# Low-part sums in columns of their own: matmuls of 348 columns in the full-width tiles of a hybrid decoder layer

## The chip, the cores and the metric

One core of a Trainium2 chip runs the program once. The metric is device microseconds of one execution, less is better. Of the engines, TensorE (PE) multiplies matrices into PSUM, VectorE (DVE) and ScalarE (ACT) do elementwise work, GpSimd (POOL) does little here, and SyncE (SP) starts transfers (DMA).

## The reference

One inference step of a decoder layer for a prompt of 512 tokens and 8 single-token samples, 520 tokens together, D = 1024, FFN width 2816, float32:

```python
mod = silu(c) @ w_ada + b_ada                    # shift, scale, gate, twice
h = _modulate(_rmsnorm(x, p["norm_pre_mix"]), sh_m, sc_m)
proj = h @ p["w_in"]                             # u | z | xBC | dt | gate_s5 | gate_ssd
ya = S5(u)           # complex diagonal state space: scan, GELU, half-GLU (w_glu)
yb = SSD(z, xBC, dt) # Mamba-2: conv, chunked scan, gated rmsnorm
merged = g_a * (ya @ p["w_branch_s5"]) + g_b * (yb @ p["w_branch_ssd"])
x = x + gt_m * _rmsnorm(merged @ p["w_out"], p["norm_post_mix"])
h = _modulate(_rmsnorm(x, p["norm_pre_ffn"]), sh_f, sc_f)
gu = h @ p["w_ffn_in"]
f = (jax.nn.silu(gu[..., :D_FF]) * gu[..., D_FF:]) @ p["w_ffn_out"]
x = x + gt_f * _rmsnorm(f, p["norm_post_ffn"])
```

The outputs are x for both groups and the new states of S5, SSD and the convolution.

## The kernel before

**The dense products.** Features lie on the 128 partitions, tokens along the free axis, in two halves of HT = 260. Weights and activations are float32, and each is split in a high part (`hi`, `whi`, of the type fp32r) and the rest (`lo`, `wlo`). A product is then three passes, hi x whi + lo x whi + hi x wlo. The helper `product` (L1148) makes them for one block of 128 input features (a k-step) of one tile of 128 output features: for a tile of full width six matmuls of 260 columns, three into each half's PSUM bank. The profile gives all of them one line, L722, that of the helper `mm` (L716), and shows fp32r as f32; `pm` is one of two pairs of main banks (2 x 512 words), `bank` one of four single banks for side work.

**The tiles.** The loop at L1068 goes through the tiles in a fixed list: u (8) and dt, the gates ga and gb (16), for each of four groups B, C, four xs and four z (40), glu (8), bs5 (8), bssd (8, with 16 k-steps), then w_out and the first FFN tiles for one half of the tokens at a time, 36 FFN tiles (fg, fu) in full width, six of the output product fo in full width with 22 k-steps, and the last two of them in halves. The pairs `pm` alternate. `evac` (L1376) reads a finished tile's sums, and is issued after the first k-step of the next tile: for gates, B, C and xs by a copy on ScalarE of all 520 columns (L696), for z and glu by an activation, for the others by VectorE.

**Weights.** A chunk of 1024 columns is fetched (`wload`), cast to `whi` on ScalarE, and its rest `wlo` made on VectorE (1.0 and 1.2 us in the profile), three chunks ahead at most.

**Side work.** S5, SSD, the modulation and the norms are generators that issue operations between k-steps (`tick`). They use VectorE, ScalarE, single banks and some matmuls.

**The order.** Every helper records its operation with an estimated cost. At the end `Plan.order` plays the recording through as a list schedule by longest way to the end, several times with perturbed priorities, and takes the best. Its result is the fixed order of instructions on each engine. The matmuls of a k-step stay together (`main`, L755).

**The end.** The last two fo tiles run in halves of 264 and 256 tokens (`cutp`), and `rstd_last` (L1645) spreads the last 256 reciprocal deviations over the partitions with two diagonal matrices of 128.

Of the kernel before, what the change touches and what calls it, by code (L numbers as in the profile page):

```python
# [16 lines left out]
NP, NS = 512, 8  # L17
T = NP + NS
HT = T // 2
KD = 8  # L20
# [29 lines left out]
class Root:  # L50
    """A tile: `get` gives the real one (it may be made late); `loc` names the memory it lies in."""
# [14 lines left out]
class Ap:  # L66
    """A view of a tile: its shape and addresses at once, the real view when the operation is issued."""
# [65 lines left out]
    def cells(self):  # L133
        """Partitions, and the set of words in one of them (bits of an integer)."""
# [20 lines left out]
def fold(dims):  # L155
    """The dimensions with neighbours joined where one stride serves both."""
# [21 lines left out]
# delay in us from the end of an operation to the start of one that waits for it  # L178
# [7 lines left out]
class Line:  # L186
    """The time of one engine: busy stretches, into whose gaps operations are put."""
# [24 lines left out]
class Plan:  # L212
    """Records operations with the memory they touch, and orders them for the engines."""
# [51 lines left out]
    def remake(self, loc, fn, words):  # L265
        """The memory `loc` gets a new tile: after everything that used the old one."""
# [8 lines left out]
    def order(self):  # L275
        """The best of some schedules: by the longest way to the end, then by latest starts."""
# [38 lines left out]
    def back(self):  # L315
        """Priorities from the schedule played backwards: the time from an operation's latest start to the end."""
# [35 lines left out]
    def play(self):  # L352
        """The course of the operations, each engine taking the most urgent of those that can start."""
# [69 lines left out]
    def shift(self, t, free, cand):  # L423
        """An operation of DVE that ACT may take at time t, where that is done sooner."""
# [32 lines left out]
class Arena:  # L457
    """One run of words in a tile of one type; blocks are cut out of it first fit."""
# [39 lines left out]
class Mem:  # L498
    """A fixed float32 arena, and slots whose type (float32 or float32r) is chosen when one is empty."""
# [10 lines left out]
    def find(self, n, dt, top):  # L510
        """The place for n words: an arena index (0 = the fixed one), or None."""
# [89 lines left out]
class Builder:  # L601
    def __init__(self, tc, I, O, sb, ps, dr):
# [10 lines left out]
        self.cutp = HT  # L613
# [6 lines left out]
        self.sg, self.ffh, self.ffl = {}, [], []  # L620
# [57 lines left out]
    def relu(self, o, a, s):  # L678
        """max(a + s, 0)"""
# [1824 lines left out]
```

## Time and profile before

| | |
|---|---|
| median of 3 runs | 1202.06 us (1200.11 to 1204.35) |
| span of the profiled execution (its own time isn't listed apart) | 1193.2 us |
| median less that span | 8.9 us |
| TensorE busy | 1168.8 us, 98%, 10182 matmuls |
| VectorE busy | 814.7 us, 68% |
| ScalarE busy | 576.3 us, 48% |
| mean granted TensorE clock | 0.998 |

Busy time of TensorE is the time in which a matmul is under way. Matmuls overlap at their ends, so what one costs in a stream is the distance from its start to the start of the next, and not its duration. A clock of 1.00 is 2.4 GHz, and half of it 1.2 GHz.

### The profile page before, as it was taken

To read this page: it belongs to the slowest core of one execution; us is meant where nothing else is said; L and a number is where in the kernel's file an instruction comes from. 1 tells how busy PE (TensorE), PEld (TensorE's weight loads), DVE (VectorE), ACT (ScalarE), POOL (GpSimd) and SP (SyncE) were. 2 spreads that over 40 slices of the span, in tenths; PEclk is the share of its full clock that TensorE was granted. 3 is DMA by queue.
4 is the path that set the end of the run, shared out by engine and by line. 5 is a ranking of instruction groups with operands and counts; after the bars stand their busy time and mean duration, and the time that the engine had idled before them with its cause. 6 is when DMAs were issued, how large, how long until landed. Compare 5 with 4: busy or idle time off the path is not lost.

```text
span 1193.2 us, 24814 instructions
## 1 busy us (share of the span) xinstructions
PE 1168.8 (98%) x10182; PEld 1124.5 (94%) x10182; DVE 814.7 (68%) x1651; ACT 576.3 (48%) x981; POOL 4.9 (0%) x32
## 2 busy tenths in 40 slices
PE   8999999999999999999999999999999899999998
PEld 6899898999999999999998989999999899999997
DVE  6898989997696877868885435499576673322236
ACT  6655444357487657847853323465223222222233
POOL 0000000000000000000000000000000000000000
PEclk9999999999999999999999999999999999999999
DMA  8838698667243343355545674344566663223244
GB/s 292 278 119 219 162 215 224 180 160 208 82 134 101 114 128 125 116 175 169 188 145 201 241 268 144 129 166 147 182 217 203 198 206 104 88 81 97 83 130 135
DMA packets 118066, 195.49 MB, mean 164 GB/s; under 512 B 45856, under 2 KB 68800, under 8 KB 115648
## 3 DMA queue, kind: packets, MB, share of 16 engines
q1 hardware_dynamic: 117952, 193.90, 52.9%
q8 instruction: 80, 1.31, 0.4%
q14 instruction: 34, 0.28, 0.1%
HBM read 165.81 MB, written 23.86 MB: 159 GB/s over the span
## 4 chain that ended last, share of the span: by engine, by line
PE 79%; DMA 9%; DVE 7%; issue 1%; SPq 1%; ACT 1%; DVEq 0%; ACTq 0%
PE pm L722 64%; PE bank L722 14%; DVE s L640 4%; DMA arena<-in_ssm 3%; DVE arena L640 2%; PE bank L734 2%; DMA s<-in_w_as 1%; DMA out_ssm_s<-arena 1%; SPq L712 1%; DVE wlo L640 1%; DMA s<-in_w_in 1%; DMA ud<-s 1%; DMA s<-s 1%; DVE s L663 1%; ACT s L696 0%
## 5 line engine op out<-in xcount | busy, mean ns | idle before, releaser
L722 PE MATMUL pm<-hi,whi 128*128 128x260 f32 (+1 forms) x1856 | 497.5, 289 | 5.9 <-DVE arena L640 3.7
L722 PE MATMUL pm<-lo,whi 128*128 128x260 f32 (+1 forms) x1856 | 483.4, 282 | 0.0
L722 PE MATMUL pm<-hi,wlo 128*128 128x260 f32 x1840 | 370.4, 283 | 0.0
L722 PEld LDWEIGHTS pm<-hi,whi 128*128 128x128 f32 (+1 forms) x1856 | 349.6, 188 | 17.4 <-issue 13.0
L722 PEld LDWEIGHTS pm<-lo,whi 128*128 128x128 f32 (+1 forms) x1856 | 349.1, 188 | 0.1
L640 DVE TENSOR_TENSOR wlo<-arena,whi 128x1024 fp32r<-128x1024 f32 (+1 forms) x157 | 188.8, 1203 | 146.7 <-ACT whi L696 144.9
L722 PEld LDWEIGHTS pm<-hi,wlo 128*128 128x128 f32 x1840 | 282.9, 188 | 0.0
L696 ACT CAST whi<-arena 128x1024 fp32r<-128x1024 f32 (+1 forms) x158 | 162.6, 1029 | 197.1 <-PE pm L722 180.2
L722 PE MATMUL pm<-s,whi 128*128 128x260 f32 (+2 forms) x1128 | 184.2, 283 | 0.0
L640 DVE TENSOR_TENSOR arena<-arena 128x512 f32<-128x512 f32 (+11 forms) x299 | 140.3, 494 | 49.8 <-DMA arena<-in_ssm 29.4
L722 PEld LDWEIGHTS pm<-s,whi 128*128 128x128 f32 x1128 | 156.2, 188 | 5.1 <-issue 4.2
L722 PE MATMUL pm<-s,wlo 128*128 128x260 f32 (+2 forms) x564 | 117.2, 283 | 0.0
L722 PEld LDWEIGHTS pm<-s,wlo 128*128 128x128 f32 x564 | 88.1, 188 | 0.0
L691 ACT ACT_TABLE_LOAD x63 | 80.8, 1283 | 10.3 <-DMA s<-acd 3.5
L722 PE MATMUL bank<-s,s 128*64 128x128 f32 (+5 forms) x672 | 75.8, 282 | 5.6 <-ACT s L696 4.4
L722 PEld LDWEIGHTS bank<-s,s 128*128 128x128 f32 (+2 forms) x672 | 61.3, 164 | 10.9 <-ACT s L696 5.3
L691 ACT ACTIVATE s<-s 128x520 f32<-128x520 f32 (+10 forms) x89 | 50.0, 570 | 38.3 <-DVE s L640 17.7
L691 ACT ACTIVATE arena<-pm 128x260 f32<-128x260 f32 (+3 forms) x44 | 21.2, 489 | 92.7 <-PE pm L722 85.7
L640 DVE TENSOR_TENSOR s<-arena,s 128x520 fp32r<-128x520 f32 (+5 forms) x60 | 56.5, 948 | 10.6 <-ACT s L696 10.4
L640 DVE TENSOR_TENSOR s<-s,arena 128x8 f32<-128x8 f32 (+6 forms) x138 | 48.6, 369 | 13.8 <-ACT s L691 12.7
L722 PE MATMUL bank<-hi,s 128*128 128x260 f32 x256 | 55.5, 285 | 0.0
L722 PE MATMUL pm<-hi,s 128*128 128x260 f32 x256 | 55.0, 285 | 0.0
(122 smaller groups left out, 1265.8 us busy)
## 6 DMA issues: line engine op xcount, KB each, us to landing
arena<-in_w_in SPq DMA_DIRECT2D x59, 512.0 KB, 3.7
arena<-in_w_fi SPq DMA_DIRECT2D x44, 512.0 KB, 4.4
arena<-in_w_ada SPq DMA_DIRECT2D x12, 1024.0 KB, 7.5
arena<-in_w_fo SPq DMA_DIRECT2D x20, 512.0 KB, 3.6
arena<-in_ssmT SPq DMA_DIRECT2D x16, 512.0 KB, 4.4
s<-acd SPq DMA_DIRECT2D x16, 512.0 KB, 4.3
arena<-in_w_bssd SPq DMA_DIRECT2D x16, 512.0 KB, 5.4
arena<-in_ssm SPq DMA_DIRECT2D x32, 256.0 KB, 3.8
```

The costliest lines, as they stand in the source:

```text
L640: self.op("V", .068 + self.fs(o) / 960, lambda: self.nc.vector.tensor_tensor(out=real(o), in0=real(a), in1=real(b), op=op), [o], [a, b, *a ...
L663: self.op("V", .068 + self.fs(o) / 960, lambda: self.nc.vector.tensor_tensor_scan(out=real(o), data0=real(a), data1=real(b), initial=0.0, ...
L691: self.op("A", c, lambda: self.nc.scalar.activation(real(o), real(a), f, bias=real(bias), scale=real(scale)), [o], [a, scale, bias], None ...
L696: self.op("A", c, lambda: self.nc.scalar.copy(real(o), real(a)), [o], [a])
L712: p = self.op("S", .475 if same else .65, lambda: self.nc.sync.dma_start(out=real(o), in_=real(a)), [o], [a], None, c)
L722: self.pe(c, lambda: self.nc.tensor.matmul(real(o), lhsT=real(l), rhs=real(r), start=start, stop=stop), [o], [l, r])
L734: self.pe(.108, lambda: self.nc.tensor.transpose(real(o), real(a), real(d)), [o], [a, d])
```

## The change

High and low parts of the activations are stored side by side, for each half 260 columns of high part and then 260 of low part (`xhl`). In a full-width tile of a kind in `WIDE` one matmul with `whi` takes all 260 high columns of a half and, in the same run, the first LA = 88 of its low columns: 348 columns. The sums of low columns don't add to those of the high ones; they stand in columns 260 to 347 of the same bank. The other 2 x 172 low columns of both halves are one matmul of 344 columns into a single bank, `lob`, taken from the four for side work. The matmuls with `wlo` stay at 260 columns. The 344s of a tile's first two k-steps are held back and come with the third's (in three tiles: the first's with the second's). `evac` of such a tile now copies the two low pieces out on ScalarE, adds the high sums to them on VectorE (520 columns), and goes on from that. For gates, B, C and xs this stands in place of the copy; for the rest it is added. u, dt, w_out and all tiles in halves keep their six matmuls (three in a half). The single bank is one for all tiles, and three are left for side work. Costs in the planner change, the last halves are 260 and 260, and the last deviations take three diagonal blocks. Many lines of the whole diff only drop comments; they are left out here.

```diff
+LA = 88
+WIDE = ("ga", "gb", "B", "C", "xs", "z", "glu", "bs5", "bssd", "fg", "fu", "fo")
...
-        self.cutp = HT
...
+        self.lob, self.late = None, []
...
     def mm(self, o, l, r, start=True, stop=True):
         n, m = self.fs(r), l.shape[-1]
         if l.dtype == F32R:
-            c = max(n / 2400, .111) if m > 32 else .048
+            c = max(n / 2400 + (.0114 if n < 300 else .0025), .112)
         else:
-            c = max(n * 4 / 2400, .216) * max(m, 32) / 128 + (.021 if m <= 64 else 0.0)
+            c = max(n * 4 / 2400 + .005, .224) * max(m, 32) / 128 + (.021 if m <= 64 else 0.0)
...
-        self.hi, self.lo = [rt(KD * T, n).rearrange("p (k t) -> p k t", k=KD) for n in ("hi", "lo")]
+
+        self.xhl = rt(KD * 2 * T, "xhl")
+        self.hl = self.xhl.rearrange("p (k a c t) -> p k a c t", k=KD, a=2, c=2)
...
-                    while len(self.banks) < 2:
+                    while not self.banks:
                         self.tick()
                         self.now += 0.3
-                    self.ring4 = [self.pm[0][:, 0], self.banks.pop(), self.pm[1][:, 0], self.banks.pop()]
+                    self.ring4 = [self.pm[0][:, 0], self.lob, self.pm[1][:, 0], self.banks.pop()]
                 if kind == "fo" and idx == 8 - NLAST and halves[0] == 0:
                     self.evac(*pend)
                     pend = None
-                    self.cutp = T - 256
...
+            wide = len(halves) == 2 and kind in WIDE
+            if wide and self.lob is None:
+                while not self.banks:
+                    self.tick()
+                    self.now += 0.3
+                self.lob = self.banks.pop()
...
-                    self.product(hi, lo, kk, pn, halves, k == 0, k == nk - 1, *rhs(k))
+                    self.product(hi, lo, kk, pn, halves, k == 0, k == nk - 1, rhs(k), wide,
+                                 k > (0 if (kind, idx) in (last, ("glu", 7), ("bssd", 7)) else 1))
                 if (kind, idx) == last:
                     if k == 0:
                         self.gelu()
-                    self.split(self.hi[:, k], self.lo[:, k], self.ub.v(KD, T)[:, k])
-                if (kind, idx) == ("glu", 7) and k < 7:
+                    for i in (k - 1,) * (k > 0) + (k,) * (k == 7):
+                        self.split(self.hl[:, i], self.ub.v(KD, T)[:, i])
+                if (kind, idx) == ("glu", 7):
                     if k == 0:
                         self.evac(*pend)
                         pend = None
-                    self.split(self.hi[:, k], self.lo[:, k], self.ub.v(KD, T)[:, k])
+                    else:
+                        self.split(self.hl[:, k - 1], self.ub.v(KD, T)[:, k - 1])
...
-    def product(self, hi, lo, k, p, halves, start, stop, xh, xl):
...
+    def product(self, hi, lo, k, p, halves, start, stop, x, wide=False, flush=True):
...
         wh, wl = [a[:, 128 * k:128 * k + 128] for a in (hi, lo)]
         self.group = []
-        for n in halves:
-            s = self.span(n)
-            self.mm(p[n][:, :s.stop - s.start], wh, xh[:, s], start=start, stop=False)
-            self.mm(p[n][:, :s.stop - s.start], wh, xl[:, s], start=False, stop=False)
-        for n in halves:
-            s = self.span(n)
-            self.mm(p[n][:, :s.stop - s.start], wl, xh[:, s], start=False, stop=stop)
+        if wide:
+            w = HT + LA
+            for n in halves:
+                self.mm(p[n][:, :w], wh, x[:, n].rearrange("p c t -> p (c t)")[:, :w], start=start, stop=False)
+            for n in halves:
+                self.mm(p[n][:, :HT], wl, x[:, n, 0], start=False, stop=stop)
+            self.late.append((self.lob[:, :2 * (HT - LA)].rearrange("p (a t) -> p a t", a=2), wh, x[:, :, 1, LA:], start, stop))
+            if flush:
+                for o, w, r, f, l in self.late:
+                    self.mm(o, w, r, start=f, stop=l)
+                self.late = []
+        else:
+            for n in halves:
+                for c in range(2):
+                    self.mm(p[n][:, :HT], wh, x[:, n, c], start=start and c == 0, stop=False)
+            for n in halves:
+                self.mm(p[n][:, :HT], wl, x[:, n, 0], start=False, stop=stop)
         self.main()
...
     def evac(self, kind, i, p, halves):
         pv = p[:, :, :HT] if len(halves) == 2 else None
         sp = lambda ap: ap.rearrange("p (a b) -> p a b", a=2)
+        lb = None
+        if len(halves) == 2 and kind in WIDE:
+            lb = self.mblk(T)
+            l2 = sp(lb.v(T))
+            self.acp(l2[:, :, LA:], sp(self.lob[:, :2 * (HT - LA)]))
+            self.acp(l2[:, :, :LA], p[:, :, HT:HT + LA])
+            self.vtt(l2, l2, pv, ADD)
+            pv = l2
+            p = l2
...
-            raw = self.mblk(T)
+            raw, lb = lb, None
             rv = raw.v(T)
-            self.acp(sp(rv), pv)
...
         elif kind in ("ga", "gb"):
-            b = self.mblk(T)
-            self.acp(sp(b.v(T)), pv)
+            b, lb = lb, None
...
     def rstd_last(self):
...
+        at = [(c0, 128), (c0 + 128, 128), (T - 128, HT - 256)]
...
+        self.vts(d[:, 2], self.ident, t[:, 2, 2:3], MULT)
...
```

On TensorE in the input projection (`pm_69`, `pm_70` are the two main pairs, `whi_71` to `wlo_75` weight buffers), two k-steps before:

```order
L722 MATMUL pm_69<-hi,whi_71 128x260
L722 MATMUL pm_69<-lo,whi_71 128x260
L722 MATMUL pm_69<-hi,whi_71 128x260
L722 MATMUL pm_69<-lo,whi_71 128x260
L722 MATMUL pm_69<-hi,wlo_74 128x260 x2
L722 MATMUL pm_70<-hi,whi_72 128x260
L722 MATMUL pm_70<-lo,whi_72 128x260
L722 MATMUL pm_70<-hi,whi_72 128x260
L722 MATMUL pm_70<-lo,whi_72 128x260
L722 MATMUL pm_70<-hi,wlo_75 128x260 x2
```

And in the change, around the third k-step of a gate tile, where the held matmuls of 344 columns come (`bank_66` is the bank `lob`):

```order
L724 MATMUL pm_70<-xhl,whi_72 128x348 x2
L724 MATMUL pm_70<-xhl,wlo_75 128x260 [waits DVE_49]
L724 MATMUL pm_70<-xhl,wlo_75 128x260
L724 MATMUL pm_70<-xhl,whi_72 128x348 x2
L724 MATMUL pm_70<-xhl,wlo_75 128x260 x2
L724 MATMUL pm_69<-xhl,whi_71 128x348 x2
L724 MATMUL pm_69<-xhl,wlo_74 128x260 x2
L724 MATMUL bank_66<-xhl,whi_71 128x344 [waits Activation_49]
L724 MATMUL bank_66<-xhl,whi_71 128x344 x2
L724 MATMUL pm_69<-xhl,whi_71 128x348 x2
L724 MATMUL pm_69<-xhl,wlo_74 128x260 x2
```

A k-step has five matmuls in place of six; three of 344 columns come together behind the third k-step's others, and the first of them waits for ScalarE.

On ScalarE at gate tiles, before (`s_16`, `s_18` are blocks of tokens, `arena` holds the fetched weights):

```order
L696 COPY s_16_997<-pm_69 128x520 [waits PE_49]
L696 CAST whi_71<-arena 128x1024 [waits DMAHW2_49]
L696 COPY s_13_579<-bank_65 128x256 [waits PE_49]
L696 COPY s_16_997<-arena 128x8x63 [waits DMAHW2_49,Activation_49]
L691 ACTIVATE s_13_579<-s_13_579 128x8x2 [waits DVE_49]
L696 COPY s_18_1108<-pm_70 128x520 [waits PE_49]
L691 ACTIVATE s_14_682<-s_14_682 128x130 [waits DMAHW3_49,DVE_49]
L696 CAST whi_72<-arena 128x1024 [waits DMAHW1_49]
```

In the change:

```order
L698 COPY s_16_776<-bank_66 128x2x172 [waits PE_49]
L698 COPY s_16_776<-pm_69 128x2x88
L698 CAST whi_71<-arena 128x1024 [waits DMAHW5_49]
L693 ACT_TABLE_LOAD [waits DMAHW4_49]
L693 ACTIVATE s_13_578<-s_13_578 128x130 [waits DVE_49]
L693 ACTIVATE s_13_578<-s_13_578 128x8x5 [waits DVE_49,Activation_49]
L693 ACTIVATE s_13_578<-s_13_578 128x8x9 [waits DVE_49,Activation_49]
L698 COPY s_18_798<-bank_66 128x2x172 [waits PE_49]
L698 COPY s_18_798<-pm_70 128x2x88
L698 CAST whi_72<-arena 128x1024 [waits DMAHW3_49]
```

Each copy of 520 columns has become two, of 2 x 172 from the single bank and 2 x 88 from the main pair, ahead of the same cast of weights.

On VectorE at the first of these tiles, in the change; the addition of 128x520 that reads `pm` is new, among S5's operations and ahead of a tile of `wlo`:

```order
L642 TENSOR_TENSOR s_11_132<-s_13_578 128x64 [waits Activation_49]
L642 TENSOR_TENSOR s_13_578<-s_13_578 128x130 [waits DVE_49]
L642 TENSOR_TENSOR s_16_776<-s_16_776,pm_69 128x520 [waits PE_49,Activation_49]
L642 TENSOR_TENSOR s_13_578<-s_13_578,s_11_132 128x16x4 [waits DVE_49]
L648 TENSOR_SCALAR s_13_578<-s_13_578 128x130 [waits DVE_49]
L642 TENSOR_TENSOR s_13_578<-s_13_578 128x16x8 [waits DVE_49]
L642 TENSOR_TENSOR wlo_74<-arena,whi_71 128x1024 [waits DMAHW5_49,Activation_49]
L648 TENSOR_SCALAR s_13_578<-s_13_578 128x130 [waits DMAHW3_49,Activation_49]
L642 TENSOR_TENSOR s_11_132<-s_13_578 128x128 [waits Activation_49]
```

The addition waits for TensorE and for ScalarE's copies, and what follows on VectorE stands behind it.

## Rows read from the trace of the kernel before

**Rows 1.** The page, part 1: busy time, share of the span, instructions of each engine.

```profile
PE 1168.8 (98%) x10182; PEld 1124.5 (94%) x10182; DVE 814.7 (68%) x1651; ACT 576.3 (48%) x981; POOL 4.9 (0%) x32
```

**Rows 2.** Windows: from:to, us; busy us (instructions) by engine; clock, DMA, GB/s.

```profile
core 0: us, PE busy (x) PEld busy (x) DVE busy (x) ACT busy (x) POOL busy (x), PEclk, DMA share, GB/s
60.00:276.00 216.00, 206.94 (x1819) 201.16 (x1819) 198.37 (x428) 106.21 (x243) 2.94 (x20) 0.99 0.71 182
225.00:276.00 51.00, 50.03 (x444) 49.16 (x443) 49.85 (x79) 26.47 (x49) 0.12 (x1) 1.00 0.62 157
276.00:402.00 126.00, 126.00 (x1113) 124.82 (x1112) 94.94 (x212) 86.46 (x128) 0.39 (x1) 1.00 0.42 125
402.00:630.00 228.00, 228.00 (x2213) 216.47 (x2212) 181.10 (x415) 157.49 (x218) 0.00 (x0) 1.00 0.46 148
630.00:1000.00 370.00, 365.87 (x3017) 350.39 (x3016) 229.55 (x369) 130.38 (x212) 0.00 (x0) 1.00 0.56 188
1000.00:1160.00 160.00, 160.00 (x1335) 160.00 (x1334) 47.43 (x60) 44.90 (x73) 0.00 (x0) 1.00 0.31 94
```

**Rows 3.** The chain of waits, 840 to 1160 us: start, us, what.

```profile
844.79 45.21 PE pm L722 x378
...
954.65 203.24 PE pm L722 x1692
```

**Rows 4.** Timeline of TensorE, 1157 to 1183 us: start, us, what.

```profile
1157.61 0.28 PE L722 MATMUL pm<-s,wlo 128*128 128x264 f32 x1
...
1165.64 0.28 PE L722 MATMUL bank<-s,wlo 128*128 128x264 f32 x1
...
1174.66 0.28 PE L722 MATMUL bank<-s,wlo 128*128 128x256 f32 x1
...
1182.08 0.28 PE L722 MATMUL bank<-s,wlo 128*128 128x256 f32 x1
```

**Rows 5.** Timeline of weight loads (PEld) and matmuls at 12 us.

```profile
12.02 0.19 PEld L729 LDWEIGHTS bank<-hi 128*128 128x128 f32 x1 [0.20 <-issue]
12.13 0.19 PEld L722 LDWEIGHTS bank<-hi,whi 128*128 128x128 f32 x1
...
12.02 0.50 PE L729 MATMUL bank<-hi 128*128 128x512 f32 x1
12.36 0.28 PE L722 MATMUL bank<-hi,whi 128*128 128x260 f32 x1
```

**Rows 6.** Timeline of TensorE at 132 us, clock at half.

```profile
132.03 0.42 PE L722 MATMUL pm<-lo,whi 128*128 128x260 f32 x1
132.25 0.42 PE L722 MATMUL pm<-hi,whi 128*128 128x260 f32 x1
132.46 0.42 PE L722 MATMUL pm<-lo,whi 128*128 128x260 f32 x1
```

**Rows 7.** Groups by line and shape, DVE and ACT: busy, mean ns | idle before.

```profile
L640 DVE TENSOR_TENSOR arena<-arena,pm 128x520 f32<-128x520 f32 x31 | 21.5, 692 | 45.2 <-PE pm L722 45.1
...
L696 ACT COPY s<-pm 128x520 f32<-128x520 f32 x39 | 23.0, 590 | 17.1 <-PE pm L722 14.8 <-DMA gb<-s 1.8 <-DVE s L640 0.2
...
L696 ACT COPY s<-bank 128x292 f32<-128x292 f32 x16 | 6.3, 395 | 7.4 <-PE bank L722 4.4 <-issue 3.0
```

**Rows 8.** What ScalarE reads of the main banks, 60 to 276 us.

```profile
L696 ACT COPY s<-pm x23: 575/592/606, 77.9 to 258.6; 128x520 f32<-128x520 f32 x22, 64x520 f32<-64x520 f32 x1
...
L691 ACT ACTIVATE s<-pm x2: 606/606/606, 272.1 to 274.9; 128x520 f32<-128x520 f32 x2
```

**Rows 9.** Waits of ScalarE, 60 to 276 us: total us, times, longest.

```profile
ACT s L691 <- DVE s L640: 17.4, 8, 6.6
...
ACT arena L696 <- DVE arena L640: 5.7, 5, 1.8
...
ACT s L696 <- DVE s L663: 5.1, 2, 4.3
...
ACT arena L696 <- DVE s L663: 3.9, 2, 2.6
```

**Rows 10.** Timeline of VectorE near the end.

```profile
1184.34 0.29 DVE L646 TENSOR_SCALAR arena<-arena 128x128 f32<-128x128 f32 x1
```

More of the change, by code (lines that the diff above doesn't have):

```diff
@@ L889, in ahead, with split @@
             f(self.uses[j])
-    def split(self, hi, lo, src):
+    def split(self, hl, src, halves=(0, 1)):
+        hi, lo = [hl[:, c] if len(halves) == 1 else hl[:, :, c] for c in (0, 1)]
+        if len(halves) == 2:
+            src = src.rearrange("p (a t) -> p a t", a=2)
         self.acp(hi, src)
@@ L1044, in build @@
             for i in range(3):
-                self.product(*self.wt[i][:2], k, ps[i], both, k == 0, k == 7, self.hi[:, k], self.lo[:, k])
+                self.product(*self.wt[i][:2], k, ps[i], both, k == 0, k == 7, self.hl[:, k])
                 self.tick()
@@ L1111, in build @@
                         pend = None
-                    self.split(self.hi[:, k], self.lo[:, k], self.ub.v(KD, T)[:, k])
+                    else:
+                        self.split(self.hl[:, k - 1], self.ub.v(KD, T)[:, k - 1])
                 if (kind, idx) == ("bssd", 7):
-                    self.ygh[k].free()
-                    self.ygl[k].free()
+                    for i in (k - 1,) * (k > 0) + (k,) * (k == 15):
+                        self.ygp[i].free()
                 if (kind, idx) == ("u", NA - 1):
@@ L1164, in dt_mm @@
         for n in range(2):
-            for i, x in enumerate((self.hi, self.lo)):
-                self.mm(p[:64, n, :HT], w[:, 64 * k:64 * k + 64], x[:, k, n * HT:(n + 1) * HT],
+            for i in range(2):
+                self.mm(p[:64, n, :HT], w[:, 64 * k:64 * k + 64], self.hl[:, k, n, i],
                         start=(k + i == 0), stop=(k + i == 8))
@@ L1221, in scaled @@
         self.vtt(t, x[:, NP:], a[:, 1:9], MULT)
-        self.vcp(hh[:, NP:], t)
-        self.vtt(hl[:, NP:], t, f_(hh[:, NP:]), SUB)
+        hs, ls = [hl[:, 1, c, HT - NS:] for c in (0, 1)]
+        self.vcp(hs, t)
+        self.vtt(ls, t, f_(hs), SUB)
         ts.free()
@@ L1288, in shifted @@
             self.vtt(v, v, sh[:, k4, 1:9], ADD)
-            self.vcp(hh[:, k4, NP:], v)
-            self.vtt(hl[:, k4, NP:], v, f_(hh[:, k4, NP:]), SUB)
+            hs, ls = [self.hl[:, k4, 1, c, HT - NS:] for c in (0, 1)]
+            self.vcp(hs, v)
+            self.vtt(ls, v, f_(hs), SUB)
             self.xr[k // 4].free()
@@ L1521, in evac @@
                     self.spawn(self.boosted(self.finish(n), (H0, 0.0)[n]), 0)
+        if lb:
+            lb.free()
     @staticmethod
@@ L1718, in ygsplit @@
                 yield 0
[L1719 removed]
+            b, = yield from self.wblk([2 * T], 1, F32R)
+            hl, xk = b.v(2, 2, HT), self.xgt(k).rearrange("p (a t) -> p a t", a=2)
             w = self.vec[:, V_MNORM + k:V_MNORM + k + 1]
[L1721 to L1722 removed]
+            self.act(hl[:, :, 0], xk, AF.Copy, scale=w)
+            self.stt(hl[:, :, 1], xk, w, f_(hl[:, :, 0]), MULT, SUB)
             yield "c"
[L1724 to L1725 removed]
+            self.ygp.append(b)
             self.done.add(("yg", k))
```

90 lines of the change are left out of this document (44 added, 46 removed).

## The prediction

> **What bounds the kernel now.** I read the page's busy times first: TensorE is busy in 98% of the span, VectorE in 68%, ScalarE in 48% [rows 1]. An average hides stages, so next comes the table by windows [rows 2]. From 276 to 630 us and from 1000 to 1160 us the matmuls fill every microsecond (126.00 of 126.00, 228.00 of 228.00, 160.00 of 160.00). From 60 to 276 us, where the S5 branch runs beside the input projection, TensorE stands for 9.06 us and VectorE is the fuller of the two: 198.37 of 216.00 us, and 49.85 of 51.00 in that stretch's last part. Third, the chain of waits: it passes through hundreds of matmuls on end [rows 3]. So the time is a count of matmuls times their pace, plus what VectorE holds up before 276 us.
>
> The pace: 45.21/378 = 119.6 ns and 203.24/1692 = 120.1 ns for a matmul of 260 columns [rows 3]. At 2.4 GHz and one column a cycle, 260 columns would be 108.3 ns. The surcharge of 11.3 ns is what the change could touch, since it leaves the columns as they are.
>
> **The stream of wide tiles.** I call a block of 128 input features a k-step. Before, a full-width tile had six matmuls of 260 columns in each. Now it has two of 348, two of 260 and one of 344: 696 + 520 + 344 = 1560 columns, as 6 x 260 = 1560. The engines' order ahead of this part shows 348 and 344 in place, so the change does what it says. Wide k-steps: gates 16 x 8, B and C 8 x 8, xs and z 32 x 8, glu and bs5 16 x 8, bssd 8 x 16, fg and fu 36 x 8, fo 6 x 22, that is 128 + 64 + 256 + 128 + 128 + 288 + 132 = 1124, in 122 tiles.
>
> What the fifth matmul less is worth depends on what the surcharge belongs to, and other widths in the trace say something of that. From a matmul of 264 columns at 1157.61 us to one at 1165.64 there are 66, of 8.03/66 = 121.7 ns each; of 256 columns there are 63 from 1174.66 to 1182.08, 117.8 ns each [rows 4]. Both are 0.460 or 0.461 ns a column, like the 260 (0.460), but so small a difference of widths separates little. One matmul of 512 columns (on zeros) does more. The next weight load starts with it, between 12.125 and 12.127 us (a window that ends at the former doesn't hold the load yet, at the latter it does), and the next matmul between 12.358 and 12.360 [rows 5]: 231 to 235 ns. A surcharge of so much a column makes 512 x 0.460 = 235.5; one of 11.3 ns a matmul makes 213.3 + 11.3 = 224.6; none makes 213.3. The row is nearest the first. It is one sample, and its neighbour is a shorter matmul.
>
> So I take a pace of so much a column: 348 columns 160.1 ns, 344 columns 158.2, and a k-step of 2 x 160.1 + 2 x 119.6 + 158.2 = 717.6 ns, as 6 x 119.6 = 717.6 now. **This term is 0.** Its bounds: a surcharge of each matmul makes -11.3 ns a k-step, x 1124 = -12.7 us; one that longer matmuls don't have, -45.1 ns (worked out under the rivals), -50.7 us.
>
> **VectorE.** Each wide tile gets an addition of 128x520 with one side in PSUM; that form takes 0.692 us [rows 7]. 122 of them are 84.4 us. From 60 to 276 us ScalarE reads 22 main tiles of 520 columns by a copy and two by an activation [rows 8], so 24 wide tiles, 24 x 0.692 = 16.6 us, enter a stretch where VectorE has 216.00 - 198.37 = 17.6 us free. It would have 215.0 us to do. Packed like the last 51 us (97.7%) that needs 219.9 us, +3.9; packed like the mean of the stretch (91.8%), 234.1, +18.1. Since what idles VectorE earlier in the stretch is short waits between small steps, which a longer queue partly fills, I take a value a third of the way, **+8 us**, and keep 0 (the additions fill gaps entirely) and +18 as ends. Later the cover holds: a tile's 8 k-steps last 5.74 us, so 22 tiles add 15.2 us to 94.94 of 126, 34 add 23.5 to 181.10 of 228 (89.7%), 36 add 24.9 to 229.55 of 370, six add 4.2 to 47.43 of 160 [rows 2]. There they lie beside matmuls, and without that cover would cost their 67.8 us.
>
> **ScalarE and the one extra bank.** The remaining low-part columns of a tile stand in one single bank until ScalarE has copied them out. Copies of 292 and 520 columns take 395 and 590 ns [rows 7]; on that line 344 columns are about 0.44 us and 176 about 0.29. For 40 tiles the two replace the copy of 0.59; for 82 they are new, 82 x 0.73 = 60 us on an engine that is half idle. What matters is when the bank is free. The first three k-steps of the next tile without their 344s give 3 x (2 x 160.1 + 2 x 119.6) = 1.68 us; less 0.44, some 1.2 us in which ScalarE may be late. It is late when it stands behind an operation that waits for VectorE: before 276 us four such groups have 8, 5, 2 and 2 waits, of 17.4 + 5.7 + 5.1 + 3.9 = 32.1 us together, up to 6.6 at a time [rows 9]. That is 15% of 216 us, so three or four of 24 tiles meet one, and of its mean of 1.9 us half is left on average, within the cover; only the longest reach past it. **+1 us**, between 0 and 29 (rival three). In the three tiles that flush a k-step earlier the cover is 1.12 - 0.44 = 0.7 us, used once each. The side work has three banks left of four, and the two banks of a main tile stay taken until the addition has read them, but the other pair covers a whole tile, 5.7 us.
>
> **The end.** The last deviations get a third diagonal block; one such product takes 0.29 us [rows 10] and stands on the last path: **+0.3**. That 264 and 256 columns become 260 and 260 changes no sum of columns: 0. The splits moved one k-step later in three tiles run 0.7 us later beside matmuls that don't need them until the next tile, or the last block in the next tile's last k-step: 0.
>
> **Sum:** 0 + 8 + 1 + 0.3 = +9.3 us on the profiled span of 1193.2, so 1202.5. The median of the runs is 1202.06, 8.9 above that span; what lies around the span is left as it is: 1202.06 + 9.3 = **1211 us**.
>
> **The rivals.**
>
> One, on the other side: wide matmuls run without the surcharge. Its place is the stream after 276 us; the case for it is in the rows at half clock, where 260 columns take 132.25 - 132.03 = 0.22 and 132.46 - 132.25 = 0.21 us [rows 6], the 216.7 ns of 260 columns at 1.2 GHz with nothing on top. So the surcharge isn't part of a column as such, and something beside the column stream that at full speed just fails to fit under 260 columns might fit under 348. Then 348 columns take 145.0 and 344 take 143.3 ns, and a k-step gains 2 x 15.1 + 14.9 = 45.1 ns. The 24 tiles before 276 us, 192 k-steps, gain nothing, since VectorE is the bound there; 932 x 45.1 = 42.0 us. With the other terms 1202.06 - 42.0 + 9.3 = 1169 us. Against it stand the 512 columns [rows 5] and a pace that is the same per column at 256, 260 and 264 [rows 3, 4]. It decides the sign as soon as a k-step gains over 9.3/932 = 10 ns.
>
> The Trainium skill, TensorE: Matmul & The Clock Gate, section Back-to-back issue gap, gives for a single matmul a gap of N/1.2 ns cold and N/2.4 + 2.5 ns warm, a constant per matmul. The trace agrees cold (0.21 to 0.22 us) and disagrees warm: 119.6 ns stands where it gives 110.8. By its figures for the widths that are new here (147.5 and 145.8 ns) beside the row for 260, the time would be an estimated 1176 us.
>
> Two: the surcharge is a fixed 11.3 ns of each matmul. 932 x 11.3 = 10.5 us gained, 9.3 lost: 1201 us. The row of 512 columns is 6 to 10 ns too long for it.
>
> Three: ScalarE's lateness at the single bank is the rule. If all 24 tiles before 276 us meet one of the waits for VectorE of the largest group (17.4/8 = 2.2 us) in full, each stops TensorE 1.0 us past its cover, or up to 29 us with the cover spent on other copies: 1202 + 9 + 29 = 1240 at most, 1230 with some two thirds. Against it: the mean above.
>
> Four: VectorE takes the additions into its gaps. Then 0 to 2 us are left of the 9.3: 1203 us.
>
> **How the numbers follow.** About 0.3%, 3.6 us, is what a measurement of this kernel can tell from no change. My forecast (1206 to 1222) has 0.42, rival one 0.27, two 0.10, three 0.07, four 0.14. Faster: rival one and a little of two, 0.30. Same, 1198.5 to 1205.7: the rest of two, and four: 0.21. Slower: forecast and three, 0.49. The range takes in the forecast with VectorE's upper end (1202 + 18 + 1, and some of three) up to 1228, and rival one down to 1166; it leaves out the part of rival one in which VectorE's cost is nothing too (1151 to 1165) and most of three. The forecast's own range is 1204 to 1224.
>
> **What would show it.** In the profile after: matmuls of 348 columns about 160 ns apart, and VectorE at 97% or more from 60 to 276 us, with that stretch some 8 us longer. A spacing of 145 to 148 ns is rival one, of 156 rival two. Waits of the 344-column matmul for ScalarE would be rival three; an input projection of unchanged length rival four. The prediction is wrong if the spacing is under 158 ns, or if the stretch before 276 us doesn't grow.

## The result, and the profile after

Six runs of the changed kernel have a median of 1208.41 us (1204.5 to 1210.43), six of the kernel before beside them 1200.89 (1198.45 to 1204.35). The ratio is 1.0065, with a 95% interval of 1.0043 to 1.0086: slower by 7.5 us, where 1211 against 1202.06, 9.3 us, was forecast. The profiled execution spans 1206.0 us and took 1207.89. So 1.9 us lie around a span, and of the 8.9 us that the prediction put there for before the rest is a quick execution: the one shown spanned 1193.2, some 6 us less than that kernel's median. The two spans differ by 12.8 us, the medians by 7.5.

The page's busy times of the changed kernel, in answer to [rows 1]:

```profile
PE 1171.6 (97%) x9064; PEld 1122.9 (93%) x9064; DVE 880.8 (73%) x1720; ACT 629.1 (52%) x1231; POOL 5.3 (0%) x32
```

TensorE is busy for 2.8 us more and stands for 1206.0 - 1171.6 = 34.4 us in place of 24.4. The stages, in answer to [rows 2]:

```profile
core 0: us, PE busy (x) PEld busy (x) DVE busy (x) ACT busy (x) POOL busy (x), PEclk, DMA share, GB/s
60.00:276.00 216.00, 201.14 (x1548) 195.37 (x1549) 200.74 (x424) 104.28 (x260) 2.55 (x18) 0.99 0.66 170
225.00:276.00 51.00, 49.19 (x387) 48.07 (x386) 50.40 (x83) 24.76 (x51) 0.23 (x2) 1.00 0.51 137
276.00:402.00 126.00, 124.06 (x1006) 120.67 (x1005) 107.33 (x227) 88.24 (x161) 0.32 (x1) 1.00 0.49 152
402.00:630.00 228.00, 227.96 (x1955) 219.65 (x1954) 196.03 (x415) 172.61 (x303) 0.00 (x0) 1.00 0.41 137
630.00:1000.00 370.00, 365.21 (x2648) 346.25 (x2647) 249.89 (x409) 152.59 (x283) 0.00 (x0) 1.00 0.57 190
1000.00:1160.00 160.00, 160.00 (x1117) 160.00 (x1116) 58.98 (x74) 54.52 (x102) 0.00 (x0) 1.00 0.30 90
```

After 276 us little changes for TensorE: 1.9 us of standing before 402, none to speak of after, and what stands from 630 to 1000 us is as it was (4.8 and 4.1 us). VectorE is busier there and not full (107.33 of 126, 196.03 of 228). From 60 to 276 us TensorE stands for 14.9 us in place of 9.1. VectorE is at 92.9% in that stretch, and not at 97%. These windows are fixed in time, and the changed kernel is some 8 to 10 us behind in them; a count between equal places follows.

**The pace.** Four k-steps of the last wide tiles, in the timeline of TensorE:

```profile
1040.60 0.48 PE L724 MATMUL pm<-xhl,whi 128*128 128x348 f32 x2
...
1041.16 0.32 PE L724 MATMUL bank<-xhl,whi 128*128 128x344 f32 x1
1041.32 0.47 PE L724 MATMUL pm<-xhl,whi 128*128 128x348 f32 x2
...
1043.46 0.48 PE L724 MATMUL pm<-xhl,whi 128*128 128x348 f32 x2
```

From 1040.60 to 1043.46 us there are four k-steps of 715 ns, where the forecast had 717.6; the 344 columns take 1041.32 - 1041.16 = 0.16 us. If the two matmuls of 260 columns still take 119.6 ns each [rows 3], 1040 columns are left for 476 ns: 0.4575 ns a column, 159.2 ns for 348 and 157.4 for 344. Forecast were 160.1 and 158.2; without a surcharge it would be 145.0 and 143.3, with one of 11.3 ns a matmul 156.3 and 154.6. Four k-steps are few. A whole tile of fo, 22 k-steps, stands between these two pieces of the chain of waits:

```profile
1083.07 1.68 PE pm L724 x12
...
1098.87 1.68 PE pm L724 x12
```

That is 15.80/22 = 718.2 ns a k-step, and so are the next two tiles; with 120.1 ns for 260 columns, as before in this part [rows 3], 348 columns take 159.9 and 344 take 158.1.

**Where the time is lost.** The weight transfers are issued at nearly the same places of the main stream in both kernels. Before:

```profile
L712 SPq DMA_DIRECT2D arena<-in_w_glu x8: 327/330/333, 487.5 to 535.8; - x8
...
L712 SPq DMA_DIRECT2D arena<-in_w_out x8: 327/328/328, 717.9 to 750.6; - x8
...
L712 SPq DMA_DIRECT2D arena<-in_w_fo x30: 327/328/328, 1033.9 to 1172.4; - x30
```

After:

```profile
L714 SPq DMA_DIRECT2D arena<-in_w_glu x8: 328/333/383, 495.0 to 551.2; - x8
...
L714 SPq DMA_DIRECT2D arena<-in_w_out x8: 327/328/328, 734.6 to 766.9; - x8
...
L714 SPq DMA_DIRECT2D arena<-in_w_fo x30: 327/328/328, 1047.7 to 1185.0; - x30
```

glu's first weights are issued 7.5 us later than before, w_out's 16.7, the first of fo 13.8 and the last 12.6. So the changed kernel is furthest behind about w_out. Some of such a difference is only that side matmuls come earlier or later in it.

**Between equal places.** Two places are the same in every order: the copy of dt on ScalarE (64x520, at 77.9 us before [rows 8]), and the read-out of the 24th wide tile, with which the prediction's stretch ends. From the one to the other, before and after:

```profile
77.90:274.90 197.00, 187.94 (x1654) 182.88 (x1654) 180.15 (x351) 95.34 (x217) 1.82 (x16) 0.99 0.75 188
```

```profile
85.50:285.20 199.70, 187.49 (x1433) 182.21 (x1432) 186.15 (x355) 91.84 (x219) 1.80 (x16) 0.99 0.67 177
```

The same for the two other seeds, whose runs follow below, in us, before to after, from one profile each:

| seed | TensorE stands up to dt | from dt to the 24th tile | after it | length from dt to the 24th tile | VectorE busy in it |
|---|---|---|---|---|---|
| 149 | 6.4 to 10.1 | 9.1 to 12.2 | 9.0 to 12.2 | 197.0 to 199.7 | 180.2 to 186.2 |
| 11 | 5.7 to 10.9 | 9.2 to 9.8 | 9.3 to 16.5 | 208.3 to 193.7 | 191.2 to 183.4 |
| 12 | 5.1 to 7.5 | 6.8 to 12.8 | 6.3 to 12.0 | 203.1 to 199.7 | 185.3 to 184.5 |

TensorE stands longer in all three parts. The middle one, where the additions lie beside S5, is 2.7 us longer with seed 149, and 14.6 and 3.4 us shorter with the others.

**The start.** The first matmul of a dense product, before and after:

```profile
9.40 0.39 PE L722 MATMUL pm<-hi,whi 128*128 128x260 f32 x1
```

```profile
13.38 0.76 PE L724 MATMUL pm<-xhl,whi 128*128 128x260 f32 x4
```

It is at 9.28 to 9.86 us in all six kernels here that store high and low parts apart, and at 11.95 to 13.51 in all eight that store them side by side, with any seed and either costs, with the additions or without. Two lines of the change bear on it that the cut of the diff leaves out. The zeros for TensorE's first matmuls are 1040 columns and not 520, so the first starts at 1.75 us in place of 1.32; and the parts of a block are written for all 520 columns, and those of the 8 samples then over them, where the 512 and the 8 were written apart:

```diff
-            self.mset("G", f_(self.hi[:, KD - 1]), 0.0)
+            self.mset("G", f_(self.xhl[:, 2 * T * (KD - 1):]), 0.0)
...
-        self.act(hh[:, :NP], x[:, :NP], AF.Copy, scale=a[:, 0:1])
...
+        self.act(hl[:, :, 0], x2, AF.Copy, scale=a[:, 0:1])
```

Which of them makes how much of the 4 us isn't shown. In the profile after, TensorE's clock falls before these first products; its busy time and the clock in two windows:

```profile
6.60:10.00 3.40, 1.08 (x18) 0.69 (x19) 0.77 (x5) 1.35 (x5) 0.00 (x0) 1.00 0.99 352
10.10:13.40 3.30, 3.08 (x22) 1.41 (x21) 2.92 (x13) 2.77 (x9) 0.00 (x0) 0.50 0.94 295
```

Before it was granted in full from 7.4 to 14 us, with TensorE busy for 4.93 of 6.6.

**The extra bank.** The group of the 344-column matmuls with their idle time, in the changed kernel:

```profile
L724 PE MATMUL bank<-xhl,whi 128*128 128x344 f32 x864 | 242.6, 321 | 6.6 <-ACT s L698 5.6 <-ACT arena L698 1.0
```

TensorE stood 6.6 us for ScalarE in front of them, 5.6 of them between dt and the 24th tile, in an engine that stood 34.4 us in all. With seeds 11 and 12 it is 5.3 and 9.6 in that part. This is more than the whole of what standing grew by there (3.2, 0.7 and 6.0), so other waits have become fewer. How that comes about, in two places of the timeline:

```profile
165.50 0.27 ACT L693 ACTIVATE s<-s 128x72 f32<-128x72 f32 x1 [0.75 <-DVE s L642]
165.68 0.42 ACT L698 COPY s<-bank 128x344 f32<-128x344 f32 x1
...
189.08 1.24 ACT L698 COPY s<-arena 128x512 f32<-128x512 f32 x2 [2.51 <-DMA ud<-s]
...
190.23 0.74 ACT L698 COPY s<-bank 128x292 f32<-128x292 f32 x2
...
191.03 0.42 PE L724 MATMUL bank<-xhl,whi 128*128 128x344 f32 x1 [1.34 <-ACT s L698]
```

At 165.50 ScalarE has waited for an S5 step of VectorE, and copies the bank only then. At 189.08 it has waited 2.51 us for a transfer of S5's (`ud`); two copies, then one of 292 and the one of 344 columns follow, and the matmul at 191.03 has stood 1.34 us. The waits of ScalarE from 60 to 276 us, beside [rows 9]:

```profile
ACT s L693 <- DVE s L642: 21.5, 18, 3.2
ACT s L698 <- DMA ud<-s: 16.2, 6, 5.6
```

Those for VectorE have become 18 of 21.5 us in place of 8 of 17.4. Those for `ud`, six of 16.2 us and up to 5.6 at a time, were there before too, as the same view of before shows, and the prediction left them out:

```profile
ACT s L696 <- DMA ud<-s: 15.2, 6, 6.0
```

### The profile page after: what moved, and what is told of

It is laid out like the page before. It is cut to its first block, busy times and chain, and to the rows that moved or that the text cites. A ratio compares the mean times of both kernels' runs of the same rounds, so it can differ in the third digit from the quotient of the medians.

```text
span 1206.0 us, 22937 instructions
## 1 busy us (share of the span) xinstructions
PE 1171.6 (97%) x9064; PEld 1122.9 (93%) x9064; DVE 880.8 (73%) x1720; ACT 629.1 (52%) x1231; POOL 5.3 (0%) x32
## 4 chain that ended last, share of the span: by engine, by line
PE 58%; DVE 19%; DMA 15%; issue 4%; ACT 2%; SPq 1%; DVEq 0%; ACTq 0%
PE pm L724 38%; PE bank L724 19%; DVE s L642 7%; DVE arena L642 5%; DMA arena<-in_ssm 4%; DVE wlo L642 3%; DMA out_ssm_s<-arena 3%; DVE s L653 2%; DMA s<-in_w_as 1%; SPq L714 1%; PE bank L736 1%; DMA ud<-s 1%; DMA s<-s 1%; DVE xhl L653 1%; DMA s<-in_w_in 1%
## 5 line engine op out<-in xcount | busy, mean ns | idle before, releaser
L724 PE MATMUL pm<-xhl,whi 128*128 128x348 f32 (+2 forms) x1984 | 468.3, 323 | 5.2 <-ACT arena L698 3.0
L724 PE MATMUL pm<-xhl,wlo 128*128 128x260 f32 x1840 | 370.9, 283 | 0.0
L724 PEld LDWEIGHTS pm<-xhl,whi 128*128 128x128 f32 (+1 forms) x1984 | 322.5, 188 | 15.0 <-issue 7.2
L724 PEld LDWEIGHTS pm<-xhl,wlo 128*128 128x128 f32 x1840 | 318.0, 188 | 0.0
L724 PE MATMUL bank<-xhl,whi 128*128 128x344 f32 (+1 forms) x896 | 248.2, 320 | 6.6 <-ACT s L698 5.6
L642 DVE TENSOR_TENSOR arena<-arena 128x512 f32<-128x512 f32 (+10 forms) x332 | 161.5, 510 | 59.0 <-DMA arena<-in_ssm 28.2
L724 PEld LDWEIGHTS bank<-xhl,whi 128*128 128x128 f32 x896 | 156.5, 189 | 9.1 <-ACT s L698 7.1
L724 PE MATMUL pm<-s,whi 128*128 128x348 f32 (+1 forms) x608 | 142.9, 319 | 0.0
L724 PE MATMUL pm<-s,wlo 128*128 128x260 f32 x564 | 117.3, 283 | 0.0
L724 PE MATMUL bank<-s,whi 128*128 128x344 f32 (+1 forms) x348 | 94.7, 310 | 0.0
L724 PEld LDWEIGHTS bank<-s,s 128*128 128x128 f32 (+2 forms) x952 | 71.8, 150 | 11.3 <-issue 4.0
L642 DVE TENSOR_TENSOR s<-arena,s 128x520 fp32r<-128x520 f32 (+5 forms) x60 | 56.6, 947 | 13.1 <-ACT s L698 12.6
```

Source lines behind the costliest of these rows:

```text
L642: self.op("V", .068 + self.fs(o) / 960, lambda: self.nc.vector.tensor_tensor(out=real(o), in0=real(a), in1=real(b), op=op), [o], [a, b, *a ...
L724: self.pe(c, lambda: self.nc.tensor.matmul(real(o), lhsT=real(l), rhs=real(r), start=start, stop=stop), [o], [l, r])
```

## The experiments

Three theories stood at first. A: the additions on VectorE, beside S5, cost the time. B: ScalarE empties the one extra bank late. C: one side bank less holds up S5 and SSD. Two came later. D: the order that the planner happens on matters as much as the edit. E: the planner's new costs do it.

**The additions alone**, on the kernel before:

```diff
...
+        if len(halves) == 2 and kind in WIDE:
+            lb = self.mblk(T)
+            l2 = sp(lb.v(T))
+            self.acp(l2[:, :, LA:], p[:, :, LA:HT])
+            self.acp(l2[:, :, :LA], p[:, :, :LA])
+            self.vtt(l2, l2, pv, MAX)
+            pv = l2
+            p = l2
...
```

> The kernel before, six matmuls a k-step and four side banks as they were, but every full-width tile is taken out of its main banks as in the change: two copies on ScalarE (344 and 176 columns) and one 128x520 operation on VectorE that reads PSUM (a maximum with itself, which changes no value). Theory A (the additions on VectorE beside S5 cost the time): about 1208 us, +5 to +8 on before. Theory B (ScalarE empties the one extra bank late, and the 344-column matmuls stand): there is no such bank, so 1200 to 1203. Theory C (one side bank less holds up S5 and SSD): 1200 to 1202.

Measured: 1216.88 us, ratio 1.0138 (1.0122 to 1.0153), +16. That is twice what A had named, and nothing that B or C had. But the loss isn't beside S5: dt is copied at 77.6 us and the 24th tile read out from 268.7 us on, 6.2 earlier than before. It comes from 595 to 660 us, where TensorE stands 13.3 us for transfers of `in_ssmT`, at a granted clock of 0.87:

```profile
595.00:660.00 65.00, 51.66 (x617) 43.98 (x617) 52.93 (x140) 39.81 (x75) 0.00 (x0) 0.87 0.63 199
...
PE bank L724 <- DMA arena<-in_ssmT: 7.5, 5, 2.4
PE bank L724 <- DMA s<-in_ssmT: 5.8, 4, 2.0
```

The kernel before issues these 16 transfers from 274.6 to 589.2 us and waits for none; this order issues them from 584.6 to 646.1. So the run shows what an order can cost, and speaks neither for A nor against it.

**The input projection as before, the rest wide:**

```diff
-WIDE = ("ga", "gb", "B", "C", "xs", "z", "glu", "bs5", "bssd", "fg", "fu", "fo")
+WIDE = ("glu", "bs5", "bssd", "fg", "fu", "fo")
...
```

> The change, but the 64 tiles of gates, B, C, xs and z keep six matmuls and their old evacuation; glu and all after it are wide, and the extra bank is taken only at glu. All three theories put the loss before glu: 1198 to 1202 us, where 676 wide k-steps at 2 x 159 + 2 x 120 + 157 = 715 ns in place of 718 give some 2 us. If it stays at 1205 or more, the loss lies in the later tiles or in the planner's new costs, the layout side by side or the end.

Measured: 1216.7 us, 1.0133 (1.0113 to 1.0152). All three theories miss: without one addition or extra bank before glu the kernel is slower than with them. (The tiles that stay narrow are 56; 1124 - 56 x 8 = 676.)

**The held matmuls flushed later:**

```diff
-k > (0 if (kind, idx) in (last, ("glu", 7), ("bssd", 7)) else 1))
+k > (0 if (kind, idx) in (last, ("glu", 7), ("bssd", 7)) else 3))
```

> The change, but the held 344-column matmuls of a tile's first four k-steps are flushed with the fifth's, not of two with the third's, so ScalarE may be 1.1 us later before TensorE stands. Theory B: the 6.6 us that the 344s waited for ScalarE in the profile go, 1202 to 1204 us. Theory A: the waits are only where VectorE's lateness shows, and come back at the weights or at S5's matmuls: 1207 to 1209. Theory C: 1208.

Measured: 1214.56 us, 1.0114 (1.0095 to 1.0132). Against B as it was put, since the waits at the bank are hardly fewer:

```profile
L724 PE MATMUL bank<-xhl,whi 128*128 128x344 f32 x864 | 208.1, 321 | 5.6 <-ACT s L698 5.5
```

**Three side banks** in the kernel before:

```diff
...
-                    self.ring4 = [self.pm[0][:, 0], self.banks.pop(), self.pm[1][:, 0], self.banks.pop()]
+                    self.ring4 = [self.pm[0][:, 0], self.lob, self.pm[1][:, 0], self.banks.pop()]
...
+            if kind == "ga" and idx == 0:
...
+                self.lob = self.banks.pop()
```

> The kernel before, with one of the four side banks put aside from the first gate tile to the tiles in halves, as in the change, and unused meanwhile. Theory C: 1205 to 1208 us. Theories A and B: 1200 to 1202.

Measured: 1200.49 us, 0.9991 (0.9972 to 1.0009). Nothing speaks for C; but this too is one order, and the next runs show how much that alone can do.

**Other draws of the order.** An edit of any kind makes the planner's perturbed list schedule come out otherwise, so the seed was changed and nothing else, in both kernels:

```diff
-SEED = 149
+SEED = 11
```

> The kernel before with 11 in place of 149 as the seed of the planner's perturbations: the same instructions, in another order of the side work. Theory D (the order that the planner happens on sets several us, and a changed kernel draws a new one): 1195 to 1212 us, as likely as not more than 4 us from before, and more likely above, if 149 was a good draw. Theory A (the edit's own work costs the time): 1198 to 1204.

> The kernel before with seed 12. Theory D: 1195 to 1212 us, and not the same as with seed 11. Theory A: 1198 to 1204.

> The changed kernel with seed 11. Theory D: 1200 to 1218 us, so that changed kernels and kernels of before overlap. Theory A: 1206 to 1212, above both of the kernel before with other seeds.

> The changed kernel with seed 12. Theory D: 1200 to 1218 us, and not the same as with seed 11. Theory A: 1206 to 1212.

Measured, before with 11 and 12: 1191.59 us (0.9919; 0.9886 to 0.9951) and 1196.1 (0.9968; 0.9948 to 0.9989). Changed: 1206.1 (1.0055; 1.0026 to 1.0083) and 1203.96 (1.0028; 1.0012 to 1.0044). D is right that a draw moves the time, by up to 9 us in the kernel before, and wrong in two things: 149 was no lucky draw, and the medians of the two kinds don't overlap, each kind with its own planner's costs. Changed less before is 7.5, 14.5 and 7.9 us for the three seeds, 10.0 in the mean; the new costs are part of the change in this. The seed 11 of the kernel before is the quickest kernel of this study. The waits at the extra bank are in every draw; with seed 12:

```profile
L724 PE MATMUL bank<-xhl,whi 128*128 128x344 f32 x864 | 243.0, 322 | 9.7 <-ACT s L698 9.6 <-ACT arena L698 0.2
```

**The planner's costs.** New ones out of the changed kernel, out of the one with a narrow projection, and into the kernel before:

```diff
-            c = max(n / 2400 + (.0114 if n < 300 else .0025), .112)
+            c = max(n / 2400, .111) if m > 32 else .048
...
```

> The changed kernel with the planner's costs of matmuls and transposes as they were before, seed 149. Theory E (the new costs, some 10% higher for 260 columns, make the planner put off side work that then comes late): 1198 to 1203 us. Theory A (the additions and copies cost the time, whatever the order): 1203 to 1211, as the three draws so far (1204 to 1208). The draw alone is worth some 5 us either way, as seeds 11 and 12 showed on the kernel before.

> As the run with a narrow input projection (1217 us), with the planner's old costs. Theory E: 1196 to 1204 us, since without the additions before glu nothing else is left to be late. If it stays over 1210, the loss lies in the wide tiles after the projection or in the layout, and theory E falls.

> The kernel before with the planner's new costs alone. Theory E: 1205 to 1215 us. Theory A: 1191 to 1203, the spread of the three seeds.

Measured: changed kernel with old costs 1218.75 us (1.0148; 1.0113 to 1.0182), narrow projection with old costs 1205.7 (1.0052; 1.0031 to 1.0072), kernel before with new costs 1219.03 (1.0149; 1.0113 to 1.0184). For E the first has the wrong sign, the other two the right one. The new costs lose 19 us in the kernel before and 11 with the narrow projection, and they win 10 us in the changed one. So with the costs equal on both sides the rest of the change loses 18.7 us under the old ones and wins 10.6 under the new ones. The order that they lead to matters more than any single term of the prediction, and it isn't good or bad by itself. The changed kernel with old costs is the plainest case of what a bad order does: a window of it, and one matmul in its timeline:

```profile
core 0: us, PE busy (x) PEld busy (x) DVE busy (x) ACT busy (x) POOL busy (x), PEclk, DMA share, GB/s
50.00:75.00 25.00, 15.56 (x136) 11.75 (x135) 24.72 (x55) 14.73 (x44) 1.12 (x4) 0.74 0.16 27
...
63.52 1.93 PE L724 MATMUL bank<-s,s 128*32 128x256 f32 x16 [7.43 <-ACT s L659]
```

TensorE stands 9.4 of 25 us there, 7.43 of them for one small step of S5, while VectorE is at 24.72 of 25; and the granted clock of the window is 0.74. The first addition of this kernel comes at 105.6 us, so the additions have no part in this stall.

**The stream alone**, with everything else of the change:

```diff
-            lb = self.mblk(T)
-            l2 = sp(lb.v(T))
-            self.acp(l2[:, :, LA:], sp(self.lob[:, :2 * (HT - LA)]))
-            self.acp(l2[:, :, :LA], p[:, :, HT:HT + LA])
-            self.vtt(l2, l2, pv, ADD)
-            pv = l2
-            p = l2
+            pass
...
```

> The changed kernel with matmuls of 348, 260 and 344 columns, the layout, the extra bank taken and the new costs, but the evacuation of before: no copies of the low sums and no addition, so the sums in the low parts' own columns are left out of the outputs. Theory A: the kernels before with other seeds less some 3 us for the stream, 1190 to 1200. Theory E: 1203 to 1212, as the costs are the new ones.

Measured: 1209.84 us, 1.0081 (1.0051 to 1.0112): no quicker than the change with its additions. The waits at the extra bank are gone with the copies:

```profile
L724 PE MATMUL bank<-xhl,whi 128*128 128x344 f32 x864 | 243.1, 322 | 0.1
```

but TensorE stands 1211.7 - 1181.4 = 30.3 us all the same, elsewhere, and the mean clock is 0.991:

```profile
PE 1181.4 (98%) x9064; PEld 1130.4 (93%) x9064; DVE 814.1 (67%) x1639; ACT 579.6 (48%) x995; POOL 5.2 (0%) x32
```

```profile
core 0: 1211.7 us, clock 0.991
```

This speaks against A as it was put, since A expected 1190 to 1200. Beside the kernel before with the same new costs (1219.03) the wide stream is 9 us quicker; beside that with old costs it is 10 us slower.

**One account for all fourteen profiles.** Span = standing (span less TensorE's busy time) + time lost to a clock at half (one less the mean granted clock, times the span; a little of it falls in standing) + the work of the matmuls, which is the rest. In us, worked out from each profile's span, TensorE's busy time and the mean clock:

| kernel | span | standing | lost to the clock | work |
|---|---|---|---|---|
| before | 1193.2 | 24.4 | 2.4 | 1166.4 |
| before, seed 11 | 1190.9 | 24.1 | 4.8 | 1162.0 |
| before, seed 12 | 1193.1 | 18.1 | 6.0 | 1169.0 |
| three side banks | 1202.0 | 23.2 | 12.0 | 1166.8 |
| before, new costs | 1211.3 | 33.9 | 7.3 | 1170.1 |
| additions alone | 1214.7 | 37.2 | 10.9 | 1166.6 |
| changed | 1206.0 | 34.4 | 3.6 | 1168.0 |
| changed, seed 11 | 1209.2 | 37.2 | 4.8 | 1167.2 |
| changed, seed 12 | 1208.5 | 32.2 | 7.3 | 1169.0 |
| flush later | 1209.3 | 30.3 | 10.9 | 1168.1 |
| changed, old costs | 1219.1 | 39.0 | 20.7 | 1159.4 |
| narrow projection | 1214.1 | 30.2 | 12.1 | 1171.8 |
| narrow, old costs | 1204.0 | 20.9 | 14.4 | 1168.7 |
| stream alone | 1211.7 | 30.3 | 10.9 | 1170.5 |

The work is the same within 5.4 us in twelve of the fourteen, whether a k-step has five matmuls or six. The other two are 4.4 and 7.0 us under the lowest of these; in the second much of the time at half clock falls in standing, in the first it isn't explained. What differs is how long TensorE stands, and what the clock takes. Each line is one execution, and the clock differs from one execution of a kernel to the next about as much as from line to line: the kernel before with new costs had 0.983 to 0.994 in four runs, the kernel before 0.990 to 0.997 in 25. The mean leaves out the start, where no clock is on record until 4.7 to 7.4 us, in the stream alone until 14.7, and counts as full, though matmuls of 512 columns stand 0.43 us apart there; what that costs is in the work. Two of the lines behind the table:

```profile
core 0: 1202.0 us, clock 0.990
```

```profile
core 0: 1219.1 us, clock 0.983
```

## Why the prediction was right, and where its working was not

- **The stream, 0.** Right, and the most useful part: 715 to 718 ns a k-step where it was 717.6 to 720.7 (six times 119.6 and 120.1), so some 2.5 ns less, x 1124 = 2.8 us. Rival one (145 ns) and rival two (156 ns) fall with the spacing of 159. The single matmul of 512 columns [rows 5] pointed to the right law among three, and couldn't have told it alone: in five profiles, those of before with seeds 11 and 12, with three side banks, with the new costs and with the additions alone, such matmuls stand in a row at the full clock, 229 to 236 ns apart, which reaches from near rival two's 224.6 to the 235.5 of the law. The rule of the Trainium skill, TensorE: Matmul & The Clock Gate, section Back-to-back issue gap, gives 147.5 ns for 348 columns; the measured 159 decides.
- **VectorE, +8.** This step failed, though its sign of being right came: the 24th wide tile is later. What ScalarE copies by 288 us in the changed kernel:

```profile
L698 ACT COPY s<-bank x52: 293/446/618, 60.4 to 285.2; 128x344 f32<-128x344 f32 x24, 128x512 f32<-128x512 f32 x14, 128x292 f32<-128x292 f32 x12, 128x256 f32<-128x256 f32 x1
...
L698 ACT COPY s<-pm x25: 305/312/587, 85.5 to 285.6; 128x176 f32<-128x176 f32 x24, 64x520 f32<-64x520 f32 x1
```

The 24th wide tile is read out from 285.2 us on, where it was 274.9 [rows 8], 10.3 us later, for a forecast of 8 and 1. But the copy of dt, the first entry of the second row and of [rows 8], is itself at 85.5 us in place of 77.9, and the first addition comes at 97.4. So 7.6 us aren't the additions' doing. They go with the planner's costs: dt is copied at 82.5 to 86.2 us in all seven kernels with the new costs, at 84.2 in the one among them that has nothing else of the change, and at 75.1 to 78.0 in six of the seven with the old ones (the seventh, at 107.6, is the changed kernel with its stall at 56 us). From dt on 2.7 us are left, and with the two other seeds the stretch is shorter than before. The prediction took VectorE's other work there as given and added 24 x 0.692 = 16.6 us to it; what was measured is +6.0, -7.8 and -0.8 us, at 93.2, 94.7 and 92.4% of the stretch and not 97. It also took VectorE for what holds TensorE up there, where before ScalarE ended 7.3 of the 9.1 us, 4.4 of them in this row:

```profile
PE bank L722 <- ACT s L696: 4.4, 3, 1.9
```

That the additions cost 0.69 us each is right:

```profile
L642 DVE TENSOR_TENSOR arena<-arena,pm 128x520 f32<-128x520 f32 x71 | 49.1, 692 | 63.6 <-ACT arena L698 63.4
...
L642 DVE TENSOR_TENSOR s<-s,pm 128x520 f32<-128x520 f32 x51 | 35.2, 691 | 13.3 <-ACT s L698 12.9
```

- **ScalarE and the bank, +1.** Mis-sized: 6.6 us in the profile, 9.7 and 5.6 in the two others whose lines stand above, 6.3 with seed 11 and 6.9 with the old costs, against 0.1 where nothing reads the bank. What failed here is the list of waits: it took those for VectorE alone and left out those for transfers, which hold ScalarE up to 5.6 us at a time, and it set the cover against a mean wait, where the few long ones do the harm. Rival three was the right mechanism at a fifth to a third of the most that it named, 29 us.
- **The start** was in no term: the first dense product is 4.0 us later in the profile, with 3.3 us at half the clock ahead of it. What of this reaches the end isn't shown: the narrow projection with old costs starts at 11.95 us and yet copies dt at 77.7.
- **The end, +0.3.** From the start of the last matmul of fo with `wlo` to the end of the span it is 11.1 us before and 12.2 after, 11.2 and 12.0 with seed 11, 11.0 and 12.0 with seed 12: some 1 us.
- **The clock** was in no term. In the profile of before it cost 2.4 us, in other profiles of kernels with the same work up to 12. Where it was followed, it fell after TensorE had been busy for a part of the time only (1.08 of 3.40 us in the rows of the start; before, 2.02 of the 4 us to 130, and 0.50 from 130.3 to 133.6), so there a stall costs more than itself.
- **The order** was taken as given. The planner draws it anew for every edit, and seeds alone move the time by up to 9 us, costs by 10 to 19. The range of 1166 to 1228 has no term for this; it was wide for other reasons.
- **After 276 us** the cover held for most: beside 67.8 us of additions TensorE stands 3.2 us longer after the 24th tile, and 7.3 and 5.7 with the other seeds. What these come from isn't shown; the forecast was 0.

So the sum came out 1.8 us from the measured difference by luck: its first term is shown, its largest isn't found where it was put, and its term of 1 was 6 to 10. Shown are: no gain in the stream; 5.6 to 9.7 us of waits at the extra bank in each of the five profiles of kernels with a wide projection that copy it out; a loss of 7.5 to 14.5 us with the same seed on both sides, the planner's costs included. What stays open is how the loss divides between those waits, the start, the additions and the order that the new costs lead to. The additions alone cost 16 us under the old costs, by waits for transfers late in the kernel, and taking them out under the new ones gave nothing. Each of these is one draw, and a draw is worth several us. Settling it would take several seeds of the stream alone, of the additions alone and of both kernels with the same costs, or one order held fixed while the edit's parts come one by one; none of these was tried.

## What to carry to other kernels

Joining matmuls into wider ones gains nothing where the pace is a constant per column: before counting on a fixed cost per instruction, find matmuls of another width in the trace, were they on zeros, and see which law they obey; one alone can mislead by more than the laws differ. Where a planner orders the instructions, run the kernel before with two other seeds first; their spread is the least that an edit has to beat, and in this kernel a seed was worth as much as the edit. Where a changed kernel is late, measure between equal places of the stream, and not in the same window of time. A buffer that one engine empties and another waits for is sized by the longest waits of the emptying engine, for transfers too, and not by their mean.

## What the runs showed of the hardware

Matmuls of 348 columns follow each other every 159 to 160 ns, of 344 every 157 to 158 (worked out from k-steps of 715 and 718 ns), of 260 every 119.6 to 120.1 and of 512 (on zeros) every 229 to 236: 0.447 to 0.462 ns a column at a granted clock of 1.00 (2.4 GHz), where at 1.2 GHz the 260 columns take 0.21 to 0.22 us [rows 6], a column a cycle with nothing on top. Why the surcharge goes with the columns at one level and is missing at the other stays open.

The mean granted clock was 0.983 to 0.998 in the fourteen profiles, 2 to 21 us of some 1200, with the work of the matmuls nearly the same; single runs of one kernel (before, with new costs) had 0.983 to 0.994. In the window of the changed kernel with old costs shown above TensorE stood for 7.43 us, and the granted clock was 0.74.
